# Q and K of four heads per transfer, uncast, with GpSimd casts, whole-tile evacuations and all stores on one queue

## The chip, the cores and the metric

One core of one Trainium2 chip. Times are device microseconds; the kernel before was run 8 times on the chip, with a median of 1079.35 us (1076.6 to 1082.74), and one execution was profiled.

## What is computed

For each of 8 x 12 = 96 heads, the product of two 1024 x 64 matrices, with no scaling and no softmax:

```python
batch, n_heads, seq, head_dim = 8, 12, 1024, 64
np.einsum('bhid,bhjd->bhij', q, k).astype(np.float32)
```

Read: 2 x 96 x 1024 x 64 floats, 50.33 MB. Written: 96 x 1024 x 1024 floats, 402.65 MB. A head's output is 4 MB, so there are eight bytes to write for each byte to read.

## The kernel before

The loop at L44 goes over the 96 heads, one at a time. For each head:

- L47 and L48 load Q and K as two DMAs from GpSimd's queue, which cast from 32-bit to 16-bit floats on the way. Row p x 8 + t of the head goes to partition p, place t, so that a partition reads eight rows of 64 floats in one run of 2 KB. The tiles `q_sb` and `k_sb` come from a pool of 24, which is twelve heads ahead.
- PE needs the head dimension on the partitions, so it transposes by a matmul with the identity. Q goes two places at a time, four instructions (L54); K one place at a time, and each place twice, once into the upper and once into the lower 64 partitions (L56, L57), sixteen instructions. All twenty write one PSUM tile `t_ps`, in a pool of one.
- VectorE copies it to SBUF: `qT_sb` (L61) and `kT_sb` (L62), the latter with the eight places moved to the innermost dimension, so that the columns come out in the order of j.
- Sixteen matmuls (L71) of 64 x 128 by 64 x 512 make the scores, each into a PSUM tile `ps` of one bank, in a pool of six. Even places lie in partitions 0 to 63 and odd ones in 64 to 127, so neighbouring matmuls use different halves of PE's rows.
- The 16 tiles go to `o_sb` in SBUF as 32-bit floats: seven by VectorE (L78), nine by ScalarE (L82). `o_sb` holds the head, 32 KB on each partition, in a pool of five.
- L86 stores it in one DMA of 4 MB, from SP's queue for even heads and ScalarE's for odd ones.

The source gives what depends on what; a scheduler then fixes the order of instructions on each engine when the program is built, and may move them past one another. On each engine they run in that built order. A tile that is to be reused makes its next writer wait until its last reader is done.

Of the kernel before, what the change touches and what calls it, by code (L numbers as in the profile page):

```python
# [1 line left out]

# [5 lines left out]


MM_DT = mybir.dt.float16


@with_exitstack
def kernel(
    ctx: ExitStack,
    tc: tile.TileContext,
    q: bass.AP,
    k: bass.AP,
    out: bass.AP,  # L20
):
    nc = tc.nc

    B, H, S, D = q.shape
    P = 128
    NT = S // P
    assert D == 64 and S % P == 0 and NT == 8

    qf = q.rearrange("b h s d -> (b h) s d")
    kf = k.rearrange("b h s d -> (b h) s d")  # L30
    of = out.rearrange("b h i j -> (b h) i (j)")
    BH = B * H

    consts = ctx.enter_context(tc.tile_pool(name="consts", bufs=1))
    ident = consts.tile([P, P], MM_DT)
    make_identity(nc, ident)

    in_pool = ctx.enter_context(tc.tile_pool(name="in_pool", bufs=24))
    tr_pool = ctx.enter_context(tc.tile_pool(name="tr_pool", bufs=3))
    out_pool = ctx.enter_context(tc.tile_pool(name="out_pool", bufs=5))  # L40
    pt_pool = ctx.enter_context(tc.tile_pool(name="pt_pool", bufs=1, space=bass.MemoryType.PSUM))
    po_pool = ctx.enter_context(tc.tile_pool(name="po_pool", bufs=6, space=bass.MemoryType.PSUM))

    for bh in range(BH):  # L44
        q_sb = in_pool.tile([P, NT, D], MM_DT, tag="in")
        k_sb = in_pool.tile([P, NT, D], MM_DT, tag="in")
        nc.gpsimd.dma_start(out=q_sb, in_=qf[bh].rearrange("(p t) d -> p t d", p=P))  # L47
        nc.gpsimd.dma_start(out=k_sb, in_=kf[bh].rearrange("(p t) d -> p t d", p=P))  # L48

        t_ps = pt_pool.tile([P, 12, P], MM_DT, tag="pt")  # L50
        qT_ps = t_ps[:, 0:4]
        kT_ps = t_ps[:, 4:12]
        for e in range(4):
            nc.tensor.transpose(qT_ps[:, e], q_sb[:, 2 * e : 2 * e + 2], ident)  # L54
        for t in range(NT):
            nc.tensor.transpose(kT_ps[0:64, t], k_sb[:, t], ident)  # L56
            nc.tensor.transpose(kT_ps[64:128, t], k_sb[:, t], ident)  # L57

        qT_sb = tr_pool.tile([P, 4, P], MM_DT, tag="qT")
        kT_sb = tr_pool.tile([P, P, NT], MM_DT, tag="kT")  # L60
        nc.vector.tensor_copy(out=qT_sb, in_=qT_ps)  # L61
        nc.vector.tensor_copy(out=kT_sb, in_=kT_ps.transpose([0, 2, 1]))  # L62
        kT_j = kT_sb.rearrange("pp p t -> pp (p t)")

        o_sb = out_pool.tile([P, NT, S], mybir.dt.float32, tag="out")
        for n in range(2):
            for t in range(NT):
                h = (t % 2) * 64
                e = t // 2
                ps = po_pool.tile([P, 512], mybir.dt.float32, tag="po")  # L70
                nc.tensor.matmul(  # L71
                    ps,
                    qT_sb[h : h + 64, e],
                    kT_j[h : h + 64, n * 512 : (n + 1) * 512],
                )
                idx = n * NT + t
                if idx % 2 == 0 and idx < 14:
                    nc.vector.tensor_copy(  # L78
                        out=o_sb[:, t, n * 512 : (n + 1) * 512], in_=ps
                    )  # L80
                else:
                    nc.scalar.copy(  # L82
                        out=o_sb[:, t, n * 512 : (n + 1) * 512], in_=ps
                    )
        out_eng = nc.sync if bh % 2 == 0 else nc.scalar
        out_eng.dma_start(  # L86
            out=of[bh].rearrange("(p t) j -> p (t j)", p=P), in_=o_sb
        )


# [1 line left out]
_INS = ['q', 'k']  # L92
_OUTS = [((8, 12, 1024, 1024), 'float32')]


# [23 lines left out]
```

## Time and profile before

| what | value |
|---|---|
| median of 8 runs | 1079.35 us |
| the profiled execution | 1076.6 us |
| its span, first to last instruction | 1074.8 us |
| PE busy | 652.0 us (61%) |
| VectorE busy | 564.5 us (53%) |
| ScalarE busy | 469.4 us (44%) |
| GpSimd busy | 102.1 us (10%) |
| L71, 1536 score matmuls, mean | 552 ns |
| L82, ScalarE copy of 128 x 512, 864 of them, mean | 595 ns |
| L78, VectorE copy of 128 x 512, 672 of them, mean | 682 ns |
| L62, VectorE copy of 128 x 1024, 96 of them, mean | 1213 ns |
| L61, VectorE copy of 128 x 512 at 16 bits, mean | 419 ns |
| a store of 4 MB, issue to landing, median | 25.6 us (SP), 26.8 us (ScalarE) |
| a load, issue to landing, median | 34.0 us |

A busy share is an average over the whole span. A matmul's mean is from its start to its modelled end, and matmuls overlap, so a mean times a count is more than the busy time. The row of DMA digits in the page gives the busy share of the core's 16 DMA engines in 40 equal slices of some 27 us, and the row below it what they moved.

### The profile page before, as it was taken

How to read it: one execution, taken by the hardware profiler on the slowest of the kernel's cores; microseconds unless marked ns; L12 is line 12 of the kernel's file. 1: busy time of each engine (PE TensorE's matmuls, PEld its weight loads, DVE VectorE, ACT ScalarE, POOL GpSimd, SP SyncE). 2: the span in 40 equal slices, each digit the busy share in tenths (PEclk: the TensorE clock that was granted, in tenths of full speed). 3: DMA queues.
4: the chain of work that ended last, by engine and by line, in shares of the span. 5: the costliest groups of instructions: out<-in, count | busy, mean ns of one | idle time of the engine just before them, and what ended most of it. 6: DMA issues, size and time to landing. Idle time of an engine off the chain costs nothing.

```text
span 1074.8 us, 9569 instructions
## 1 busy us (share of the span) xinstructions
PE 652.0 (61%) x3456; PEld 210.3 (20%) x3456; DVE 564.5 (53%) x864; ACT 469.4 (44%) x865; POOL 102.1 (10%) x198
## 2 busy tenths in 40 slices
PE   6897157845862854497175944836818739908830
PEld 2322012211220211122021211211202212203200
DVE  5677245743761762477153743744726536717730
ACT  4476134633651652376043633634615525606640
POOL 6000002002001000020002001002001020000000
PEclk9998555655565675568555565565765555556555
DMA  9999999999999999999999999999999999999998
GB/s 231 399 416 417 431 412 363 417 428 350 425 421 361 423 424 390 394 374 419 426 392 368 418 418 381 412 426 350 419 431 384 421 341 417 425 404 377 428 430 378
DMA packets 41519, 428.44 MB, mean 399 GB/s; under 512 B 4608, under 2 KB 29184, under 8 KB 29184
## 3 DMA queue, kind: packets, MB, share of 16 engines
q1 hardware_dynamic: 6912, 201.33, 43.9%
q10 hardware_dynamic: 6912, 201.33, 43.7%
q0 software_dynamic: 27648, 25.18, 14.6%
q8 instruction: 27, 0.44, 0.1%
q14 instruction: 20, 0.16, 0.0%
HBM read 50.33 MB, written 402.65 MB: 421 GB/s over the span
## 4 chain that ended last, share of the span: by engine, by line
PE 35%; another core or an unknown queue 26%; DMA 17%; DVE 15%; issue 2%; ACT 1%; DVEq 0%; POOL 0%; POOLq 0%; ACTq 0%
PE ps L71 22%; DMA out_dram<-o_sb 9%; DMA k_sb<-in_k_dram 8%; DVE o_sb L78 8%; DVE kT_sb L62 6%; PE t_ps L56 5%; PE t_ps L57 5%; PE t_ps L54 4%; DVE qT_sb L61 1%; ACT o_sb L82 1%; DMA q_sb<-in_q_dram 0%; DVEq L78 0%; POOL ident masks.py:197 0%; ACTq L82 0%
## 5 line engine op out<-in xcount | busy, mean ns | idle before, releaser
L82 ACT COPY o_sb<-ps 128x512 f32<-128x512 f32 x864 | 468.1, 595 | 567.2 <-PE ps L71 551.8
L71 PE MATMUL ps<-kT_sb,qT_sb 64*128 64x512 f16 x1536 | 485.8, 552 | 45.8 <-DVE o_sb L78 33.4
L78 DVE COPY o_sb<-ps 128x512 f32<-128x512 f32 x672 | 427.1, 682 | 162.9 <-ACT o_sb L82 86.6
L56 PE MATMUL t_ps<-ident,k_sb 128*64 128x128 f16 x768 | 141.9, 300 | 182.9 <-DMA k_sb<-in_k_dram 182.8
L61 DVE COPY qT_sb<-t_ps 128x512 f16<-128x512 f16 x96 | 40.2, 419 | 309.0 <-PE ps L71 298.7
L54 PE MATMUL t_ps<-ident,q_sb 128*128 128x128 f16 x384 | 67.6, 276 | 155.4 <-DMA q_sb<-in_q_dram 109.5
L57 PE MATMUL t_ps<-ident,k_sb 128*64 128x128 f16 x768 | 150.5, 301 | 0.0
L71 PEld LDWEIGHTS <-qT_sb 64*128 64x128 f16 x1536 | 94.5, 105 | 202.3 <-issue 169.4
L56 PEld LDWEIGHTS <-k_sb 128*64 128x64 f16 x768 | 73.3, 143 | 239.8 <-DMA k_sb<-in_k_dram 197.8
L62 DVE COPY kT_sb<-t_ps 128x1024 f16<-128x1024 f16 x96 | 116.4, 1213 | 0.0
L57 PEld LDWEIGHTS <-k_sb 128*64 128x64 f16 x768 | 76.4, 142 | 107.2 <-issue 107.2
L48 POOL DMA_DIRECT2D k_sb<-in_k_dram x96 | 50.9, 530 | 448.2 <-PE ps L71 130.4
L47 POOL DMA_DIRECT2D q_sb<-in_q_dram x96 | 51.0, 532 | 420.7 <-DMA q_sb<-in_q_dram 164.4
L54 PEld LDWEIGHTS <-q_sb 128*128 128x128 f16 x384 | 31.3, 112 | 275.8 <-issue 141.9
L82 ACT ACT_TABLE_LOAD x1 | 1.3, 1283 | 0.7 <-PEq L103 0.7
masks.py:199 POOL TENSOR_SCALAR_AFFINE_SELECT ident<-ident 128x128 f16<-128x128 f16 x1 | 0.3, 304 | 0.1
masks.py:197 POOL MEMSET ident<- 128x128 f16 x1 | 0.2, 204 | 0.3 <-POOLq L103 0.3
L103 POOL MEMSET const-float32-0.0<- 128x1 f32 x1 | 0.1, 98 | 0.2 <-issue 0.2
L103 POOL MEMSET const-bfloat16-1.0<- 128x1 bf16 x1 | 0.1, 101 | 0.0
L103 POOL MEMSET const-uint8-127<- 128x1 uint8 x1 | 0.1, 101 | 0.0
L103 POOL MEMSET const-float32-1.0<- 128x1 f32 x1 | 0.1, 98 | 0.0
## 6 DMA issues: line engine op xcount, KB each, us to landing
out_dram<-o_sb SPq DMA_DIRECT2D x48, 4096.0 KB, 25.6
out_dram<-o_sb ACTq DMA_DIRECT2D x48, 4096.0 KB, 26.8
q_sb<-in_q_dram POOLq DMA_DIRECT2D x96, 128.0 KB, 34.0
k_sb<-in_k_dram POOLq DMA_DIRECT2D x96, 128.0 KB, 34.1
```

The source lines that it names most:

```text
L47: nc.gpsimd.dma_start(out=q_sb, in_=qf[bh].rearrange("(p t) d -> p t d", p=P))
L48: nc.gpsimd.dma_start(out=k_sb, in_=kf[bh].rearrange("(p t) d -> p t d", p=P))
L54: nc.tensor.transpose(qT_ps[:, e], q_sb[:, 2 * e : 2 * e + 2], ident)
L56: nc.tensor.transpose(kT_ps[0:64, t], k_sb[:, t], ident)
L57: nc.tensor.transpose(kT_ps[64:128, t], k_sb[:, t], ident)
L61: nc.vector.tensor_copy(out=qT_sb, in_=qT_ps)
L62: nc.vector.tensor_copy(out=kT_sb, in_=kT_ps.transpose([0, 2, 1]))
L71: nc.tensor.matmul(ps, qT_sb[h : h + 64, e], kT_j[h : h + 64, n * 512 : (n + 1) * 512],)
L78: nc.vector.tensor_copy(out=o_sb[:, t, n * 512 : (n + 1) * 512], in_=ps)
L82: nc.scalar.copy(out=o_sb[:, t, n * 512 : (n + 1) * 512], in_=ps)
L103: nc = _bacc.Bacc("TRN2", target_bir_lowering=False, num_devices=1)
```

## The change

All of it is in the kernel's function. Part by part:

**Blocks.** Heads are worked on in blocks of 2 x G: G is 1, 1, 2 and then 4 eleven times, so that the blocks are of 2, 2, 4 and 8 heads. A block's first G heads form its half 0, the others its half 1.

**Loads** are four per block (Q and K of each half), uncast, from the queues of SP and ScalarE. Each takes G whole heads as one run: 2 KB on a partition for G = 1, 8 KB for G = 4 (then 1 MB in all). The twelve loads of the first three blocks go into a buffer of the output pool that isn't yet in use (`early`), and three of block 3 are issued ahead of the loop. All later ones are on ScalarE's queue, into raw tiles in a pool of three.

**Casts** are GpSimd copies, four per block, that put the two halves side by side: 64 values of half 0, then 64 of half 1. The tile `half_sb` has one buffer, which blocks 0 to 2 share, and each later block has it to itself.

**Transposes** take 128 columns, both halves at once, 16 for a set (8 for Q, 8 for K); a set is G x 8 rows' worth of columns, and a block has G sets, for 2 x G heads. VectorE copies a set with two instructions of 128 x 1024, which scatter the columns over the block's heads. The transposed tiles of a block are in a pool of two, so that the next block's sets can be made while this block's scores run; in the source they are placed one after each head.

**Scores.** A head of half 0 uses partitions 0 to 63 for all its matmuls, one of half 1 uses 64 to 127. Two matmuls fill a PSUM tile of two banks (pool of three), and one instruction of 128 x 1024 copies it: VectorE for three of the eight tiles, ScalarE for five.

**Stores** are all on SP's queue. The output pool has four buffers in place of five.

```diff
+    sizes = [1, 1, 2] + [GMAX] * (BH // (2 * GMAX) - 1)
...
+    in_pool = ctx.enter_context(tc.tile_pool(name="in_pool", bufs=3))
+    half_pool = ctx.enter_context(tc.tile_pool(name="half_pool", bufs=1))
+    tr_pool = ctx.enter_context(tc.tile_pool(name="tr_pool", bufs=2))
+    out_pool = ctx.enter_context(tc.tile_pool(name="out_pool", bufs=4))
...
+        def load(self, n, eng, raw=None):
+            if raw is None:
+                x_sb = in_pool.tile([P, self.elems], F32, tag="x")
+                raw = x_sb
+            self.raw[n] = raw
+            start = (self.first + n // 2 * self.G) * S
+            src = (qf, kf)[n % 2][start : start + self.G * S]
+            eng.dma_start(out=raw, in_=src.rearrange("(p r) d -> p (r d)", p=P))
...
+        def cast(self, n):
+            nc.gpsimd.tensor_copy(
+                out=self.halves[n % 2][:, :, n // 2],
+                in_=self.raw[n].rearrange("p (r d) -> p r d", d=D),
+            )
...
+        def transpose(self, a):
+            G, pp = self.G, P // self.G
+            t_ps = pt_pool.tile([P, 2 * NT, P], F16, tag="pt")
+            for x, src in enumerate(self.halves):
+                for t in range(NT):
+                    nc.tensor.transpose(t_ps[:, x * NT + t], src[:, a * NT + t], ident)
...
+            nc.vector.tensor_copy(
+                out=qT[:, :, :, :, a],
+                in_=t_ps[:, :NT].rearrange("c t (g m) -> c g t m", g=G),
+            )
+            nc.vector.tensor_copy(
+                out=kT[:, :, :, a],
+                in_=t_ps[:, NT:].rearrange("c t (g m) -> c g m t", g=G),
+            )
...
+        def scores(self, n):
+            half, g = divmod(n, self.G)
+            cs = slice(half * D, (half + 1) * D)
...
+            o_sb = out_pool.tile([P, NT, S], F32, tag="out")
+            for t in range(NT):
+                ps = po_pool.tile([P, S], F32, tag="po")
+                for j in range(2):
+                    js = slice(j * 512, (j + 1) * 512)
+                    nc.tensor.matmul(ps[:, js], qT[cs, g, t], kT[cs, g, js])
+                if t in (1, 4, 6):
+                    nc.vector.tensor_copy(out=o_sb[:, t], in_=ps)
+                else:
+                    nc.scalar.copy(out=o_sb[:, t], in_=ps)
+            nc.sync.dma_start(
...
+    def refill(i):
+        b = blocks[i] if i < len(blocks) else None
+        c = blocks[i + 1] if i + 1 < len(blocks) else None
+        if b:
+            half_sb = half_pool.tile([P, 2 * half_elems], F16, tag="half")
+            b.place(half_sb, 0)
+            for n in range(3):
+                b.cast(n)
+        yield
+        if b:
+            b.load(3, nc.scalar)
+            b.cast(3)
+        if c:
+            c.load(0, nc.scalar)
+            c.load(1, nc.scalar)
+        yield
+        yield
+        if c:
+            c.load(2, nc.scalar)
...
+        for n in range(2 * b.G):
+            b.scores(n)
+            for job in todo:
+                next(job, None)
+            if nxt and done < nxt.G:
+                nxt.transpose(done)
+                done += 1
+                if done == nxt.G and i > 0:
+                    todo.append(refill(i + 2))
+                    next(todo[-1])
```

In the order that is built, the transposes don't stand one after each head. With heads counted from 0 and their tiles from 0 to 7, PE's order for a block of eight, heads 16 to 23, is this (set 5.1 is set 1 of block 5, q and k its two halves):

```
h16: tiles 0 1 2, sets 5.1 and 5.2, tiles 3 4 5 6 7
h17: tiles 0 1 2, set 5.3, set 6.0 q, tile 3, set 6.0 k, tiles 4 5 6 7
h18 to h23: tiles only
```

The seven blocks that begin with heads 24, 32 and so on up to 72 have the same order. ScalarE's queue has the last load of block 6 and the first of block 7 ahead of head 17's first copy, and two more loads of block 7 within head 17 and ahead of head 18. In the first blocks the sets stand closer: set 2.1 in heads 2 and 3, sets 3.0 to 3.3 in heads 4 to 6, 4.0 in heads 6 and 7, 4.1 to 4.3 in heads 8 and 9, 5.0 in head 9; the last load of block 3 is issued within head 3, that of block 4 ahead of head 6, that of block 5 ahead of head 9.

## The prediction

> **What bounds the kernel now.** I read the slices first, then the DMA queues, then short windows, then the waits, and last the groups.
>
> ```profile
> DMA  9999999999999999999999999999999999999998
> GB/s 231 399 416 417 431 412 363 417 428 350 425 421 361 423 424 390 394 374 419 426 392 368 418 418 381 412 426 350 419 431 384 421 341 417 425 404 377 428 430 378
> ...
> q1 hardware_dynamic: 6912, 201.33, 43.9%
> q10 hardware_dynamic: 6912, 201.33, 43.7%
> q0 software_dynamic: 27648, 25.18, 14.6%
> ...
> HBM read 50.33 MB, written 402.65 MB: 421 GB/s over the span
> ```
>
> The DMA engines never rest, whereas no compute engine is over 61% busy. q1 and q10 are the stores of SP and ACT, q0 the loads of GpSimd. The shares add to 102%, since packets overlap a little.
>
> ```profile
> 120.00:140.00 20.00, 1.97 (x19) 1.13 (x21) 0.00 (x0) 0.58 (x1) 0.53 (x1) 0.50 1.02 426
> 164.00:173.00 9.00, 5.94 (x33) 2.18 (x33) 3.77 (x6) 3.73 (x8) 4.29 (x9) 0.50 1.18 251
> 1040.00:1070.00 30.00, 0.00 (x0) 0.00 (x0) 0.00 (x0) 0.00 (x0) 0.00 (x0) 0.50 1.00 431
> ```
>
> The columns are PE, PEld, DVE, ACT, POOL, clock, DMA share, GB/s. The last window holds stores alone: 431 GB/s. From 120 to 140 us compute stands still and stores go on at 426 with a trickle of loads. From 164 to 173 us the stores have mostly run out and loads fill the engines; the 251 counts the two-byte side that lands in SBUF, so about twice that is read. Compute comes in fits, the DMA doesn't.
>
> ```profile
> ACT o_sb L82 <- PE ps L71: 551.8, 363, 29.5
> DVE qT_sb L61 <- PE ps L71: 298.7, 46, 29.3
> PEld L56 <- DMA k_sb<-in_k_dram: 197.8, 26, 19.7
> PE t_ps L56 <- DMA k_sb<-in_k_dram: 182.8, 17, 19.5
> ```
>
> PE waits up to 19.7 us for one k tile while the stores still have work. Those waits cost little here: some byte is always moving. So what counts is total DMA work, plus any time in which neither a load nor a store is in flight.
>
> **What the Trainium skill says.** "DMA: Bandwidth & Descriptors", Queues, rings and completion order: each DMA engine goes round-robin between the queues that have work. The trace agrees: a k tile is 8 packets per engine, a 32 KB store packet takes about 1.2 us (43.9% of 1074.8 us over 384 per engine), and 8 x (2 x 1.2 + 0.1) = 20 us is the 19.7 us wait. The same page, Measured, gives 425 GB/s for a 16 MB load; no load of such runs is in this trace. "GPSIMD Engine Reference", Elementwise side-by-side cycle accounting: about 1.8 cycles of 1.2 GHz per element for a tight loop; the trace shows no GpSimd copy. "TensorE: Matmul & The Clock Gate", Part 3: a weight load overlaps a running matmul only in another row group. Before, L71 alternates the halves, and eight matmuls take 2.15 us at 201 us, 0.27 each; what one half alone does isn't shown.
>
> **The change part by part.**
>
> Stores: the same 402.65 MB in the same 4 MB pieces, all on SP. From 20 to 25 us, with SP's first store nearly alone on the engines, 423 GB/s move, so one store queue is about as fast as two: 402.65 / 0.431 = 934 us, unchanged.
>
> Loads: 192 casting loads in 2 KB runs become 12 early ones and 44 of 1 MB in 8 KB runs. Old cost: 1074.8 - 934 - 4 (2.6 until the first packet, 1.5 after the last) = 137 us, or 367 GB/s of what is read. New cost, bounds: 137 us if runs don't matter, 117 at the stores' rate. I take the page's 425: 50.33 / 0.425 = 118 us. Saving 19.
>
> GpSimd loses 102 us of descriptor work and gets the casts: 98,304 elements per partition; at 1.8 cycles 1.5 ns each, 148 us in all, 3 us for a 2048-element cast (bounds 1.8 at one cycle, 4.5 at 2.6). Hidden by volume, not in its chain, below.
>
> PE: transposes fall from 20 to 8 per head (16 per set, 48 sets; about 0.11 us each, four of L54 taking 0.61 with 0.28 the length of one). A head's 16 matmuls are now all in one row half: 0.27 each if weight loads still hide, 0.54 if halves gave all the overlap; 4.3 to 8.6 us, I take 6.5. ACT: five copies of 1024. Bounds 595 (L82) and 1190; with the ScalarE page's 0.83 ns per element, 595 + 427 = 1022 ns, 5.1 us a head. DVE: three copies at L62's 1213 ns, 3.6 us, and 2.4 in a head with a set. So a head takes 6.5 us, 8.3 with a set, against 1052 / 96 = 11.0 us of DMA. All three engines lie under the DMA by volume, and four output buffers let them run ahead by three stores.
>
> Now the chain that volume doesn't show. The half tile has one buffer, so the casts of block i+2 wait for the last transposes of block i+1. Raw tiles have three, so the fourth load waits for the first of those casts, and its issue stands on ACT ahead of copies. By the built order PE is also in line: behind the first Q transposes (which need three casts) and K transposes (which need the fourth) stand the next matmuls. The fourth load shares engines with a queued store: 8 x (1.2 + 0.3) + 2 = 14 us.
>
> In the steady blocks (head 17, 25, ...): the last set is transposed about a microsecond before head 13's store lands (time 0). First cast done at 2, load issued, landed at 16, cast at 19, K transposes 20, four more tiles and copies 25, first store packet 27. Queued then: three stores, 28, and two loads, 5, less 1.5 of landing delay: until 31. Covered by 4 us. A 4.5 us cast eats 3 of it. Cost taken: 0.
>
> At the start nothing is queued yet. Early loads, 7.3 MB, keep DMA busy from 2.2 to 19.3 us. Block 0's casts end near 8, transposes and copies at 11.5, head 0 at 19.5, first packet 21.5: gap 2. Heads 1 to 3 end at 27.5, 34.5, 41.5. Block 3's first cast follows block 2's last transpose (35.5) at 38.5; its fourth load, issued 39.5, lands 53.5, is cast 56.5; three sets between copies bring head 4 out at 67, packets 69.5. Stores 0 to 3 and three loads end at 21.5 + 37.4 + 6.5 = 65.4: gap 4. Head 6 waits likewise for block 4's casts (out at 92, packets 94, engines empty near 92: gap 2), head 9 for block 5's (134.5 against 131.5: with delay and the loads beside it, gap 3). After it heads lead. Sum 11; I take 10, bounds 0 and 25.
>
> Sum: 2.2 start + 934 + 118 + 10 + 1.5 tail = 1066 us of span. The profiled execution took 1076.6, 1.8 over its span, and stands 2.7 below the median of 1079.35. So 1066 + 1.8 + 2.7 = 1070.5; forecast 1070 us.
>
> **The rivals.**
>
> A. No gaps: casts of 1.8 us, or early loads and stores interleave well. For it: in every slice before, something was in flight. Against it: the chain at heads 4 to 9 meets queues not yet full. Time 1070 - 10 = 1060.
>
> B. Loads don't get cheaper: a byte read costs what it did, whatever the run. For it: with loads alone (10 to 15 us) 191 GB/s land, so 382 are read, and longer runs may do no better. Against: the engines' share there is 1.19, a sign of many small packets, and the balance over the span says 367. Time 1070 + 19 = 1089 with the early gaps whole; but then the loads in flight last longer and fill about half of them and of the rest of the difference, so 1079.
>
> C. The in-order chain decides, slower. Place: PE at the K transposes of a block's first set, behind the fourth load and its cast, with ACT stuck at that load's issue. It decides once head 17's first packet comes later than the 31 us of queued DMA. With 4.5 us casts (+3, since the first and the last stand in the chain) and PE at 8.6 us a head (+3: the last set ends later, and so do the four tiles behind) it comes at 33: 2 us in each of eight steady blocks, 16. The early gaps, which hang on the same chain, double to 20. Time 1070 + 16 + 10 = 1096. For it: the page gives no figure for a casting copy, and one row half alone is untested. Against: 4 us of cover.
>
> **How the numbers follow.** Forecast 0.56, A 0.12, B 0.11, C 0.21. What differs by under 0.2% (1077.2 to 1081.5) can't be told from no change. The forecast, 1060 to 1080 by its early gaps, is faster in nine tenths, 0.51, same in the rest, 0.04, bar 0.01 slower; A adds 0.12 faster; B splits into 0.03 faster, 0.05 same, 0.03 slower; C 0.02 same, 0.19 slower. Together 0.66, 0.11, 0.23. The range runs from 1058 (no gap, loads at the stores' rate) to 1093, which leaves out the upper half of C and little else.
>
> **What would show it.** Right: loads' share near 11% in place of 14.6; GB/s of about 430 in nearly every slice after the fifth; slices two to six a little lower; ACT and DVE waiting at the first copy of a head for an output store to land. Wrong on the chain: waits of PE for GpSimd (half tile) over 20 us every eighth head, with DMA digits below 9. Wrong on PE: a group of 1536 matmuls whose busy time nears the span. Wrong on loads: all slices at 9 and GB/s near 420. The prediction falls if casts take over 4.5 us, or if a single store queue leaves holes between its 4 MB pieces.

## The result: slower by half a per cent

The kernel after takes 1085.29 us (median of 11 runs, 1083.28 to 1085.7), the kernel before, in the runs beside it, 1078.84 us (median of 32). The ratio is 1.0057, with an interval of 1.0042 to 1.0072. The forecast was 1070 us and faster; the time lies between the bounds of 1058 and 1093, but it went the other way. The profiled execution took 1084.45 us over a span of 1082.7, against 1076.6 and 1074.8.

From the page of the kernel after, the slices, the DMA queues and the bytes:

```profile
DMA  9999999999999999999999999999999999999998
GB/s 368 416 378 358 418 369 432 430 425 435 435 406 421 428 433 432 429 427 397 436 428 414 432 435 425 409 433 433 423 429 431 401 436 426 427 430 436 428 429 373
...
q1 hardware_dynamic: 14976, 406.85, 87.6%
q10 hardware_dynamic: 6912, 46.14, 11.0%
...
HBM read 50.33 MB, written 402.65 MB: 418 GB/s over the span
```

The loads' queue (q10, with the early loads of SP counted in q1) has the 11% that was forecast, down from 14.6, and the DMA digits are all 9. By these lines alone the change did what it should. But a digit of 9 means 90% or more of some 27 us, and the second row has dips to 358 to 378 in slices three, four and six and shallower ones later. A slice hides a hole of two microseconds, so short windows have to be read.

The windows of the kernel after (columns as before; DMA share and GB/s are the last two):

```profile
66.00:73.00 7.00, 5.25 (x20) 1.75 (x18) 5.82 (x4) 1.11 (x2) 0.00 (x0) 1.00 0.76 293
...
138.00:149.00 11.00, 9.50 (x34) 3.86 (x35) 3.67 (x3) 4.97 (x5) 2.82 (x2) 1.00 0.85 293
...
315.00:327.00 12.00, 7.74 (x24) 3.06 (x25) 3.67 (x3) 3.95 (x4) 1.89 (x1) 1.00 0.96 356
1040.00:1070.00 30.00, 5.32 (x13) 1.42 (x10) 3.67 (x3) 4.96 (x5) 0.00 (x0) 1.00 1.01 435
```

The last line is the stores at full rate, as before. In the first two the stores have run out (in the second their last packets end at 139.4 us). What is left in flight is loads of the one load queue, and they move 293 GB/s with the engines at a share of 0.76 and 0.85. Before, loads left alone kept the engines over-full: from 10 to 15 us their share was 1.19 and 382 GB/s were read, as the prediction has it.

The mean of 293 hides two states. Here is the beginning of the first window again, cut where the packets of a load end:

```profile
65.50:68.25 2.75, 2.53 (x11) 0.87 (x9) 2.00 (x1) 0.18 (x1) 0.00 (x0) 1.00 1.00 414
68.25:70.00 1.75, 0.22 (x3) 0.22 (x4) 1.75 (x3) 0.83 (x1) 0.00 (x0) 1.00 0.49 108
```

While the packets of a load follow one another, loads alone move 414 GB/s. At 68.4 us the load's packets are through; the next one was issued at 68.1, and until its packets follow one another the engines stand half empty. So the queue is not slow here: nothing was queued behind the load in flight. A second cause adds to it: from 144.5 to 149 us two loads are in flight, and 251 GB/s move, because packets that mostly take 0.31 us take up to 1.1. What makes them long is not shown. In the whole trace the packets of 8 KB on the load queue take 311 ns on average in microseconds that are at least half filled by stores, and 361 in the others; the median is 309 in both.

The groups of the kernel after that replace the assumed durations (busy us and mean ns of one stand behind the bar):

```profile
L129 ACT COPY o_sb<-ps 128x1024 f32<-128x1024 f32 x480 | 472.7, 1014 | 567.8 <-PE ps L125 420.7
L125 PE MATMUL ps<-kT,qT 64*128 64x512 f16 x1536 | 665.0, 625 | 58.5 <-ACT o_sb L129 41.7
L127 DVE COPY o_sb<-ps 128x1024 f32<-128x1024 f32 x288 | 352.2, 1223 | 451.7 <-PE ps L125 387.0
...
L84 POOL CAST half_sb<-x_sb 128x2048 f16<-128x2048 f32 x44 | 82.1, 1893 | 753.7 <-PE t_ps L98 621.1
L106 DVE COPY qT<-t_ps 128x1024 f16<-128x1024 f16 x48 | 110.8, 2307 | 87.3 <-PE t_ps L98 87.3
```

No engine is near the span. The cast takes 1.9 us where 3 was taken, 665.0 / 96 = 6.9 us of matmuls per head where 6.5 was taken, and only the scattering copy of Q is far off, 2307 ns for 1213.

The waits of the kernel after (us in total, times, longest):

```profile
PEld L98 <- POOL half_sb L84: 191.3, 23, 15.2
PE t_ps L98 <- POOL half_sb L84: 177.3, 20, 14.3
POOL half_sb L84 <- DMA x_sb<-in_k_dram: 132.6, 11, 14.4
...
ACT o_sb L129 <- DMA out_dram<-o_sb: 76.1, 28, 3.6
ACT o_sb L129 <- POOL half_sb L84: 70.9, 10, 8.0
```

The first three are one chain: eleven times a cast waits up to 14.4 us for the fourth load, and PE's transposes wait up to 14.3 us for that cast. ACT waits for an output store to land only 28 times: most heads aren't ahead of the stores.

The timeline of the kernel after at the block of head 24 shows one turn of it (start, duration, engine, line, operation, the idle time before it and what ended it):

```profile
294.77 1.89 PE L98 MATMUL t_ps<-ident,half_sb 128*128 128x128 f16 x16
...
296.78 5.57 POOL L84 CAST half_sb<-x_sb 128x2048 f16<-128x2048 f32 x3 [68.54 <-PE t_ps L98]
298.70 0.33 ACTq L72 DMA_DIRECT2D x_sb<-in_k_dram  x1
...
301.05 1.93 ACT L129 COPY o_sb<-ps 128x1024 f32<-128x1024 f32 x2 [7.72 <-POOL half_sb L84]
...
316.80 1.89 POOL L84 CAST half_sb<-x_sb 128x2048 f16<-128x2048 f32 x1 [14.45 <-DMA x_sb<-in_k_dram]
...
318.75 1.03 PE L98 MATMUL t_ps<-ident,half_sb 128*128 128x128 f16 x8 [14.34 <-POOL half_sb L84]
...
320.78 1.22 DVE L127 COPY o_sb<-ps 128x1024 f32<-128x1024 f32 x1 [19.48 <-PE ps L125]
```

The last set ends at 296.7, the first cast at 298.7, the fourth load is issued at once, its cast begins 18.1 us later, and the K transposes stand at the head of PE's order all that while. The first packet of head 25's store comes at 328.7; the stores before it ended at 322.9.

**The account of the span.** From the start and duration of every DMA packet in the traces I worked out, in bins of 1 us and as a mean over the 16 engines, how long the engines had work (packets that overlap count twice, up to the whole bin), how long they stood idle before the last bin in which at least half of them worked, and what was idle in the tail behind that. Time to the last packet is the sum of the three. The traces don't tell which engine a packet ran on, so that overlap on one engine can hide idle time of another. The last column counts the bins of which stores fill less than a twentieth.

| kernel | to the last packet | DMA work | idle, of it between 4 us and the tail | idle in the tail | bins without stores, after 20 us |
|---|---|---|---|---|---|
| before | 1073.5 | 1068.4 | 3.9, 0.5 | 1.2 | 53 |
| after | 1082.8 | 1064.8 | 14.6, 12.4 | 3.3 | 48 |

So 10.7 us of idle time and 2.1 of tail came, and the loads became cheaper by 3.6 us where 19 had been forecast.

### The profile page after: what moved, and what is told of

The parts are those of the page before. It is cut to its first block, busy times and chain, and to the rows that moved or that the text cites. A ratio compares the mean times of both kernels' runs of the same rounds, so it can differ in the third digit from the quotient of the medians.

```text
span 1082.7 us, 6240 instructions
## 1 busy us (share of the span) xinstructions
PE 754.6 (70%) x2304; PEld 286.6 (26%) x2304; DVE 509.6 (47%) x384; ACT 473.9 (44%) x481; POOL 91.5 (8%) x62
## 4 chain that ended last, share of the span: by engine, by line
DMA 39%; PE 36%; DVE 11%; issue 4%; POOL 4%; ACT 2%; POOLq 0%; ACTq 0%; SPq 0%; DVEq 0%
PE ps L125 28%; DMA out_dram<-o_sb 25%; DMA x_sb<-in_k_dram 14%; PE t_ps L98 8%; DVE qT L106 5%; POOL half_sb L84 4%; DVE o_sb L127 3%; DVE kT L110 3%; ACT o_sb L129 2%; DMA early<-in_q_dram 0%; POOLq L226 0%; ACTq L129 0%; SPq L72 0%; DVEq L127 0%; POOLq L84 0%
## 5 line engine op out<-in xcount | busy, mean ns | idle before, releaser
L129 ACT COPY o_sb<-ps 128x1024 f32<-128x1024 f32 x480 | 472.7, 1014 | 567.8 <-PE ps L125 420.7
L125 PE MATMUL ps<-kT,qT 64*128 64x512 f16 x1536 | 665.0, 625 | 58.5 <-ACT o_sb L129 41.7
L127 DVE COPY o_sb<-ps 128x1024 f32<-128x1024 f32 x288 | 352.2, 1223 | 451.7 <-PE ps L125 387.0
L125 PEld LDWEIGHTS <-qT 64*128 64x128 f16 x1536 | 209.4, 139 | 473.9 <-issue 462.9
L98 PE MATMUL t_ps<-ident,half_sb 128*128 128x128 f16 x768 | 95.3, 311 | 235.0 <-POOL half_sb L84 177.3
L98 PEld LDWEIGHTS <-half_sb 128*128 128x128 f16 x768 | 77.2, 143 | 286.8 <-POOL half_sb L84 191.3
L106 DVE COPY qT<-t_ps 128x1024 f16<-128x1024 f16 x48 | 110.8, 2307 | 87.3 <-PE t_ps L98 87.3
L84 POOL CAST half_sb<-x_sb 128x2048 f16<-128x2048 f32 x44 | 82.1, 1893 | 753.7 <-PE t_ps L98 621.1
L110 DVE COPY kT<-t_ps 128x1024 f16<-128x1024 f16 x48 | 59.3, 1236 | 0.0
L84 POOL CAST half_sb<-early 128x512 f16<-128x512 f32 (+1 forms) x12 | 8.8, 755 | 5.6 <-DMA early<-in_q_dram 5.4
```

What stands on the lines that cost most here:

```text
L84: nc.gpsimd.tensor_copy(out=self.halves[n % 2][:, :, n // 2], in_=self.raw[n].rearrange("p (r d) -> p r d", d=D),)
L98: nc.tensor.transpose(t_ps[:, x * NT + t], src[:, a * NT + t], ident)
L106: nc.vector.tensor_copy(out=qT[:, :, :, :, a], in_=t_ps[:, :NT].rearrange("c t (g m) -> c g t m", g=G),)
L110: nc.vector.tensor_copy(out=kT[:, :, :, a], in_=t_ps[:, NT:].rearrange("c t (g m) -> c g m t", g=G),)
L125: nc.tensor.matmul(ps[:, js], qT[cs, g, t], kT[cs, g, js])
L127: nc.vector.tensor_copy(out=o_sb[:, t], in_=ps)
```

## The experiments

All ratios are to the kernel before in the same session. The DMA account of each run is in a table at the end of this section.

**The fourth load taken out of the chain.** It goes to a tile of its own, as a casting load from GpSimd's queue, issued with the third instead of behind the first cast. Two things come with it: three loads instead of four share the three raw tiles, so that each tile comes free a cast sooner for the next block, and in the built order some of PE's sets stand elsewhere in heads 4 to 10. From head 16 on PE's order is the same.

```diff
+            elif raw == "16":
+                x16_sb = x16_pool.tile([P, self.elems], F16, tag="x16")
+                raw, eng = x16_sb, nc.gpsimd
...
         if b:
-            b.load(3, nc.scalar)
             b.cast(3)
...
             c.load(2, nc.scalar)
+            c.load(3, None, "16")
```

> The fourth load of each block goes, two heads earlier, into a 16-bit tile of its own by a casting DMA on GpSimd's queue, so that it no longer waits for a cast. Chain theory (last set, first cast, fourth load behind stores, its cast, K transposes, all in PE's order): some 15 to 18 us of waiting go out of each steady block and out of heads 4, 6 and 9, so of 25 us without enough DMA work about half stays, all of it early; some 1072 us, ratio to the kernel before 0.993. Row-half theory (PE is too slow with one half of its rows) and scatter theory (the Q copies of 2307 ns are what holds PE up): unchanged, 1085 and 1.005.

It took 1071.74 us, ratio 0.994 [0.9918, 0.9961]. Its waits:

```profile
ACT o_sb L133 <- DMA out_dram<-o_sb: 190.9, 53, 5.9
...
PE t_ps L102 <- POOL half_sb L88: 72.3, 13, 15.1
```

PE's wait for the casts falls from 177.3 to 72.3 us, and ACT's wait for stores rises from 76.1 to 190.9: the heads are ahead of the stores now, which is the state the forecast had taken for granted. Taking the load out of the chain gains 13.5 us (12.6 by the two ratios), more than the whole loss. That the load casts on the way is not what gains: a packet of it, 8 KB read, takes 322 ns (median), an uncast one 309.

The packets show where the gain comes from. In the kernel after, each of the heads 17, 25, 33, 41, 49, 57 and 65 is preceded by a hole in the stores, of 1.4 to 5.8 us; here none of them is. When head 12's stores end, this kernel is 7.2 us ahead of the kernel after and has read 1 MB more; when head 74's end, with all loads in on both sides, it is 17.9 us ahead. So roughly half comes from the early heads, where the sets moved too, and half from the steady blocks, where PE's order is the same. The tail takes 4 us of it back.

**Q copied in runs.** The scattering copy writes each set's 32 columns side by side in place of one in every four; the rows of the output come out in another order.

```diff
-                "c (g t m a) -> c g t m a", g=G, t=NT, a=G
+                "c (g t a m) -> c g t a m", g=G, t=NT, a=G
...
-                out=qT[:, :, :, :, a],
+                out=qT[:, :, :, a],
```

> VectorE writes the transposed Q in runs in place of every fourth element; the rows of a head come out in another order. Scatter theory: the copies fall from 2307 to about 1200 ns and the gaps by half, 1073 us. Chain theory: three of these copies stand in a block's chain, so some 3 us come off each chain; 1079 to 1082 us, ratio 1.000 to 1.003.

It took 1086.65 us, ratio 1.009 [1.0063, 1.0117]. The group in this kernel:

```profile
L106 DVE COPY qT<-t_ps 128x1024 f16<-128x1024 f16 x48 | 33.1, 689 | 89.8 <-PE t_ps L98 89.8
```

The copy falls from 2307 to 689 ns, 78 us in all, and nothing is gained. The chain's small gain didn't come either: the scheduler put some sets elsewhere, the idle time of the steady blocks at head 24 went, and other places lost more (head 9's store came at 152.9 us in place of 149.7). A shorter copy in the chain is not settled by this run, since the order moved with it.

**Stores on two queues again**, SP for even and ScalarE for odd heads.

```diff
-            nc.sync.dma_start(
+            (nc.sync, nc.scalar)[n % 2].dma_start(
```

> Odd heads are stored from ScalarE's queue, where the loads are. Theory of the single queue (one queue leaves holes between its 4 MB pieces): 1072 us or less. Chain theory: a load now stands in line behind a store on its own queue, and takes its turn against another, so it lands 10 us later or more; slower than the changed kernel, 1095 to 1120 us, with longer waits of PE for the half tile.

It took 1099.62 us, ratio 1.022 [1.0184, 1.0257]. The cast's wait for the fourth load in this kernel:

```profile
POOL half_sb L84 <- DMA x_sb<-in_k_dram: 187.5, 11, 19.3
```

The wait for the fourth load grows from 132.6 to 187.5 us over the same eleven times, 5 us each. But the load doesn't land later than before by sharing the engines, as was expected: from issue to landing the eleven fourth loads take 12.7 us on average, against 15.6 in the kernel after. They are issued later. The block of head 24 in this kernel:

```profile
309.07 5.57 POOL L84 CAST half_sb<-x_sb 128x2048 f16<-128x2048 f32 x3 [66.12 <-PE t_ps L98]
...
319.58 0.35 ACTq L72 DMA_DIRECT2D x_sb<-in_k_dram  x1
```

The first of the three casts ends at 311.0, and the load goes out 8.6 us after it, behind output copies of ScalarE; in the kernel after it goes out at once. The scheduler put sets and loads elsewhere in every block of this kernel. So a chain made longer goes with a slower kernel again, and the theory of the single queue gets no support; what two store queues cost by themselves this run doesn't separate.

**Matmuls that alternate between PE's row halves**, as before. The odd tiles of a head take their operands from the other half, thus from another head's data; the count and shape of everything stay, and so does PE's order.

```diff
+                cs = slice((half + t) % 2 * D, ((half + t) % 2 + 1) * D)
```

> Tiles of a head take the two halves of PE's rows in turn, in the same built order; a head's odd tiles are then those of the other half's head. Row-half theory: PE's score matmuls fall from about 0.4 to 0.27 us apart, heads from 6.5 to 5 us, the gaps by two thirds; 1068 us. Chain theory: matmuls get faster likewise, but they are 4 to 5 us of a chain of some 38, so 1078 to 1083 us.

It took 1076.4 us (20 runs), ratio 0.9985 [0.9972, 0.9998]. Its matmul group:

```profile
L126 PE MATMUL ps<-kT,qT 64*128 64x512 f16 x1536 | 533.6, 607 | 164.8 <-ACT o_sb L130 113.6
```

PE's busy time falls from 665.0 to 533.6, 1.4 us per head, and the time by about 9 us (8 by the ratios), which lies between the two expectations. By the store packets 6.5 us of it are there when head 12 ends. The row half matters, though PE was idle for 30% of the span in the kernel after (754.6 us busy). The granted clock is not what tells these kernels apart: it was 1.00 in the kernel after and 0.61 in the profile of the faster kernel before, and of the twenty executions here, which took 1075.13 to 1078.45 us at 0.51 to 1.00, the one at 1.00 took 1077.81.

**Both at once**, the early fourth load and the alternating halves, asks whether PE's speed counts by itself.

```diff
+                cs = slice((half + t) % 2 * D, ((half + t) % 2 + 1) * D)
...
-            b.load(3, nc.scalar)
...
+            c.load(3, None, "16")
```

> The early fourth load and the alternating halves together. If PE's speed matters by itself (heads 4 to 9, where nothing is queued), both savings add: 13 + 9 us off, 1063. If it matters as a part of the chain alone, little is left for it once the load is out of it: 1069 to 1071.

It took 1069.5 us, ratio 0.9929 [0.9901, 0.9957]: 2 us under the early load alone, not 9, and the intervals of the two overlap. As far as these runs can tell, PE's speed counts as a link of the chain and not by itself.

**The late loads on GpSimd's queue**, so that ACT's and PE's order has no load issue in it.

```diff
-            b.load(3, nc.scalar)
+            b.load(3, nc.gpsimd)
...
-            c.load(0, nc.scalar)
-            c.load(1, nc.scalar)
+            c.load(0, nc.gpsimd)
+            c.load(1, nc.gpsimd)
...
-            c.load(2, nc.scalar)
+            c.load(2, nc.gpsimd)
```

> All loads after the first fifteen go out from GpSimd's queue, uncast, each behind the cast that frees its raw tile; ScalarE issues none. The built order then puts a block's first K set one head later. Chain theory: the load still waits for the first cast, but ScalarE copies on and PE has another head to work on, so the steady gaps go (10 us) and the early ones shrink; 1070 us, ratio 0.993. If ScalarE's and PE's standing in line is not what costs, 1084.

It took 1083.2 us, ratio 1.0053 [1.0033, 1.0072], within 2 us of the kernel after; the 1070 expected by the version of the chain that puts the cost on ACT's order didn't come. A window of it:

```profile
90.00:95.00 5.00, 0.97 (x3) 0.07 (x1) 1.76 (x2) 1.01 (x1) 1.20 (x1) 1.00 0.13 57
```

The load stays behind the first cast, and now behind the two other casts on GpSimd too: it goes out 3.6 us after the first (10.1 at head 6, where the engines fall to a share of 0.13). In the steady blocks, with the K set a head later, the holes in the stores are gone. Yet between the ends of head 12 and of head 74, with the same bytes moved at both, this kernel gains only 1.2 us on the kernel after; between 820 and 910 us the engines now stand idle for 3.2 us in place of 1.9. So taking ACT's standing at the load's issue away (70.9 us of waits in the kernel after) doesn't bring the 13 us. As the order moved and the load went out later, it isn't shown to cost nothing.

**Casting loads in 8 KB runs**: no casts, no tile of halves, no raw tiles. GpSimd issues the same blocks, two blocks ahead, straight into 16-bit tiles (eleven buffers), and PE transposes each half by itself, 32 instructions per set.

```diff
+                nc.gpsimd.dma_start(
+                    out=x, in_=src.rearrange("(p r) d -> p r d", p=P)
                 )
...
+                    for h in range(2):
+                        nc.tensor.transpose(
+                            t_ps[h * D : (h + 1) * D, x * NT + t],
+                            self.x[2 * h + x][:, a * NT + t],
+                            ident,
+                        )
```

> Loads of four heads in 8 KB runs go out from GpSimd's queue and cast on the way, into eleven 16-bit tiles; no casts, no half tile, no raw tiles, no loads on ScalarE's queue; PE transposes 64 columns at a time, twice as many. With the whole chain gone, nothing but the first heads should lie open: 1052 us for all bytes at 431 GB/s, 3 to start, 2 at the end, and 3 to 6 of early gaps make a span of 1061 and a time of some 1064, ratio 0.986. If what is lost comes instead from PE's speed or from one store queue, it stays near E1's 1072 or above.

It took 1070.85 us, ratio 0.9934 [0.9908, 0.9959]. From its page:

```profile
DMA  9999999999999999999999999999999999999997
...
q1 hardware_dynamic: 13824, 402.66, 88.0%
q0 software_dynamic: 8064, 25.17, 12.0%
```

Without the chain the idle time in the middle is 1.1 us, and the kernel is faster than before. It still misses the expected time: the engines' work is 1059.8 us in the table below where 1052 was taken, and 7.2 us are idle in the tail where 2 was taken. This run and the early fourth load, whose intervals overlap, leave nothing of the computation out, and both beat the kernel before and the kernel after.

**The price of the loads by itself.** Two kernels leave most loads out. In the kernel before, heads 12 to 95 use the tiles of the first twelve again:

```diff
+        if bh < 12:
...
+            kept.append((q_sb, k_sb))
+        q_sb, k_sb = kept[bh % 12]
```

> The price of the old loads by itself. Only the first twelve heads are loaded; heads 12 to 95 use those tiles again, so 44.04 of the 50.33 MB aren't read and most outputs are those of other heads. If a byte read costs what the prediction's balance gave it (137 us for 50.33 MB, 2.72 us per MB), 120 us go: about 959. If the packets of the old loads lie partly beside others on the DMA engines, so that they cost some 127 us in all (154 engine-microseconds less the 26 that overlap), 111 us go: about 968.

In the kernel after, the blocks from head 16 on cast block 3's raw tiles again:

```diff
+            if self.first >= 16:
+                self.raw[n] = blocks[3].raw[1 + n % 3]
+                return
```

> The price of the new loads by itself. Blocks from head 16 on cast again what block 3 loaded, so 41.94 of the 50.33 MB aren't read and most outputs are those of other heads; casts, sets, matmuls and stores stay. At the prediction's 118 us for 50.33 MB, 98 us go; at the 126 that the packet times give, 105. The fourth load also leaves the chain in every block from head 16 on, so by the chain theory the steady gaps (about 5 us of the 14) go too: 982 by the prediction's price, 975 by the packets'. The gap ahead of head 4 stays. By the rival that the loads matter only as part of the chain and cost no more than predicted, 982 or above.

They took 978.83 us, ratio 0.9081 [0.9055, 0.9107], and 994.04 us, ratio 0.9222 [0.9191, 0.9253]: 20 and 12 us above the first figures that were expected. Neither difference is the price of the loads. The end of the first, in windows:

```profile
945.00:950.00 5.00, 0.00 (x0) 0.00 (x0) 0.00 (x0) 0.00 (x0) 0.00 (x0) 0.50 1.00 433
...
960.00:965.00 5.00, 0.00 (x0) 0.00 (x0) 0.00 (x0) 0.00 (x0) 0.00 (x0) 0.50 0.06 26
```

From about 956 us to the end a sixteenth of the full rate goes on (share 0.06, 26 of 433 GB/s): by that, one engine of the sixteen is still busy with its share. And a window of the second, around its early blocks:

```profile
120.00:140.00 20.00, 14.24 (x47) 5.28 (x46) 10.71 (x8) 7.24 (x8) 7.41 (x4) 0.50 0.68 289
```

With few loads left to fill them, its early holes are wider: 22.9 us of idle from 4 to 160 us, against 8.1. The account takes both apart:

| kernel | to the last packet | DMA work | idle, of it between 4 us and the tail | idle in the tail | bins without stores, after 20 us |
|---|---|---|---|---|---|
| fourth load early | 1068.9 | 1057.1 | 4.9, 2.7 | 6.9 | 14 |
| Q in runs | 1085.4 | 1064.1 | 18.3, 16.3 | 3.1 | 28 |
| two store queues | 1095.3 | 1073.7 | 19.7, 17.8 | 1.9 | 27 |
| alternating halves | 1075.1 | 1062.7 | 8.8, 7.0 | 3.7 | 33 |
| early and alternating | 1066.9 | 1057.6 | 3.0, 0.7 | 6.3 | 4 |
| loads on GpSimd | 1078.7 | 1063.7 | 13.7, 11.5 | 1.3 | 18 |
| casting loads | 1070.9 | 1059.8 | 3.9, 1.1 | 7.2 | 4 |
| before, few loads | 975.5 | 954.0 | 3.6, 0.6 | 17.8 | 0 |
| after, few loads | 992.3 | 957.5 | 25.3, 23.3 | 9.6 | 16 |

The old loads cost (1068.4 - 954.0) us for 44.04 MB, or 385 GB/s, 131 us for all. The new ones in the kernel after cost (1064.8 - 957.5) for 41.94 MB, 391 GB/s, 129 us. With the fourth load early the same loads, three quarters of them as in the kernel after, cost (1057.1 - 957.5), 421 GB/s, 120 us. "DMA: Bandwidth & Descriptors", Measured, of the Trainium skill has 425 for a load of 16 MB, which the prediction took, and 341 for one of 1 MB, the size of these loads. The price of the loads lies between the two, near the first where another load or store is in flight beside them.

## Why the prediction was wrong

**What held.** The bound was named rightly: DMA work plus time in which the engines have nothing. Stores cost 937 us by the account (957.5 less 8.39 MB at 421 GB/s), 3 more than the 934. One store queue is enough (435 GB/s from 1040 to 1070 us); the kernel with two was slower, in another built order. ScalarE and VectorE evacuate at 1014 and 1223 ns, as taken. Rival A (no gaps) falls with the 12.4 us of idle time, rival B (loads no cheaper, 1079) has the loads right by outcome, but by another cause.

**The step that failed** is the cover of the chain: "Cost taken: 0" in the steady blocks, and only what is idle counted in the early ones. With it fell the load term of 118 us. Place and links were those of rival C; taking one link out gives 13.5 us. Two things were wrong in it.

The first is its length. For the block of head 24 against the prediction's table, with head 21's store landing near 290 us by its packets (the last one ends at 289.0):

| link | predicted, us | measured, us |
|---|---|---|
| last set transposed after that landing | -1 | about 6.7 |
| first cast done | 3 later | 2.0 later |
| fourth load, issue to landing | 14 | 18.0 |
| landing to cast done | 3 | 2.0 |
| K transposes | 1 | 1.1 |
| four tiles, copies, first store packet | 7 | 8.9 |
| first store packet | 27 | about 38.7 |

The cast, the cost that worried me most, was shorter than taken. The first link is two thirds of the error of 11.7 us, the fourth load's landing a third: the last set doesn't come as soon as its output buffer is free, because PE's order puts the matmuls of a head and the copies of the set before ahead of it, in one row half at 6.9 us a head and with a Q copy of 2.3 us. The alternating halves shorten this link and the last. Against the chain stood the queued stores, which ended at 322.9, some 33 us after that landing, where the working had 31 with the loads: it took 28 us for three stores and 37.4 for four, where its own 934 us over 96 stores make 29.2 and 38.9. So the cover was about what had been taken, and the chain outlasted it. It did so in all seven blocks from head 17 to head 65, by 1.4 to 5.8 us.

The second is what a hole costs. The working said that only time "in which neither a load nor a store is in flight" is lost, read off a kernel in which loads alone kept the engines over-full: in its 53 us without stores 383 GB/s were read. (Twice the 251 of the prediction's window is too much, since stores run in a part of it.) In the kernel after, 48 us pass without stores; 6.1 of them are idle, and the loads in them move some 300 GB/s. The early fourth load cuts the 48 to 14, and DMA work falls by 7.7 us along with 9.7 of idle, while the tail rises by 3.6: together the 13.9 us between the two traces. That loads alone are what costs is in part argued: with the late loads on GpSimd's queue 18 us pass without stores, and the DMA work is still 1063.7.

**The terms of the sum**, predicted against measured in the trace of the kernel after: start and gaps 12.2 against 14.6, stores 934 against 937, loads 118 against 128, tail 1.5 against 3.3; that is 17 us over a span of 1066. The early idle time, 10 forecast, is 8.1 up to 160 us and the steady blocks add 4.3. By size the loads are the largest miss, and with the early fourth load 8 of their 10 us go, which points to the chain again. The other part of the forecast saving of 19 was never there: the old loads cost 131 and not 137, and the new ones 120 at best.

**The chances.** C had 0.21, to be decided by casts of 4.5 us and PE at 8.6 us a head. It was decided without either, and at 1085 in place of 1096, because loads filled most of the holes in the stores: 8.1 us are idle in the early heads and 4.3 in the steady blocks, where C had put 20 and 16.

## What to carry to other kernels

Where DMA is the bound, look for the one transfer that can be issued only after a compute step and whose result stands in an engine's fixed order: it is worth a buffer to take it out of that place, even where it is one transfer in four of a stream that is a ninth of the bytes. Time a chain from where its first link really stands in the engine's order, not from when its buffer comes free. Don't count a hole in the stores as filled because a load is in flight, since a load with nothing queued behind it leaves a hole at its end: compare the rate and the DMA share of the loads alone in a short window, since a slice's digit of 9 hides both.

## What the hardware showed that was not expected

- Loads of 8 KB packets from one queue moved 414 GB/s alone while packets followed one another, but 293 over windows of 7 and 11 us in which one load ended before the next was under way. The old casting loads in 2 KB runs, alone, read 382 to 383 at a share of 1.2. What loads moved alone hung here on what was queued behind each, and on long packets whose cause is open.
- A GpSimd cast of 128 x 2048 from 32 to 16 bits takes 1893 ns, 0.92 ns per element. The prediction's estimate of 1.5 came from the 1.8 cycles in "GPSIMD Engine Reference" of the Trainium skill, Elementwise side-by-side cycle accounting. The same section has 1.03 cycles for its smallest loop bodies, an estimate of 0.86 ns at 1.2 GHz, which is the nearer one; the measurement decides.
- The same VectorE copy of 128 x 1024 at 16 bits took 2307 ns with its output at every fourth element and 689 ns in runs.
- Kernels whose stores don't pause in their last 100 us can end unevenly: 6.9 and 7.2 us of mean idle in the tail of the early fourth load and the casting loads, 9.6 and 17.8 with few loads. In the kernel before with few loads the share is 0.06, one engine of sixteen, for the last 18 us. What delays that engine is not shown.
